# An output projection turned around: weights stationary, 512 tokens moving, split weights re-read from DRAM

## The chip, the cores and the metric

One Trainium2 chip, one core. The metric is device time in microseconds of one execution of the whole kernel. A run's time lies a little above the span that the profile shows (from the first to the last instruction).

## The reference

One decoder layer over 2048 tokens of width 1024, all in float32:

```
h   = rms_norm(x, g_mix)
mix = rwkv7_time_mix(h @ rw_in ...)          # 768 columns, a delta-rule scan over the tokens
mem = memory_cross_attention(q_mem, kv)      # 256 columns, 4 heads into 256 memory tokens
x   = x + concat(mix, mem) @ w_out           # the output projection: (2048 x 1024) @ (1024 x 1024)
u   = rms_norm(x, g_ffn) @ w_ff1
x   = x + square(relu(u)) @ w_ff2            # 1024 -> 4096 -> 1024
```

The change touches the line with `w_out` alone.

## The kernel before

A float32 product is made of three TensorE products. `split` (L89 to L96) writes an operand as a high part (ScalarE rounds it to fp32r, L92) and a low part (VectorE subtracts, L93); high by high, high by low and low by high are then summed in PSUM.

The tokens are in four groups of 512. The kernel has three stretches in time.

- `project` (L634) makes the input projection of a group: 22 blocks of 128 columns, each with 24 matmuls of 512 moving tokens (L102, PSUM tile `pz`), the weights being the stationary operand. Group 0 splits the weights and keeps both parts in DRAM (`w_d`); the later groups load the parts with four DMAs of 256 KB per block (L655). Six blocks of a group are turned back to token rows by four TensorE transposes (L688) and a copy (L690).
- The delta-rule scan works through 16 pairs of chunks of 64 tokens (`prepare`, `scan`, `post`); the result of a pair goes to the DRAM tile `mix_d` (L566). Beside it, as filler, run the projections of later groups, the cross-attention (`mem_attention`, result in `mem_d`), and the output projection `output` (L808). `dense` (L111) gives the filler's steps priorities that lie a few pairs behind the scan. From the priorities a planner writes the order of every engine before the kernel runs.
- The MLP (`prologue`, `layer1`, `layer2`) is dense TensorE work from about 1520 us to the end. The first `prologue` norms the rows of groups 0 and 1 and splits them into tiles that take the memory that the earlier stretches give back.

`output(g, parts)` loads the group's `mix_d` and `mem_d` rows (tile `mt`, L817 to L820) and splits them into `xh` and `xl` (one pair of tiles for each half of the 1024 inputs). For each quarter of 256 output columns, `weights256` (L612) loads four tiles of `w_out` (L617) and splits them into eight tiles `wo`. Then `rows_mm` (L624) makes, for each part of 256 tokens, 48 matmuls in which 128 tokens are the stationary operand and 256 weight columns move (L629, PSUM tile `pout`). The result has token rows already: VectorE adds `x` (L834) and one DMA stores it to `x2_d` (L835). Groups 0, 1 and 2 are done in one call with both parts; group 3 in two calls of one part each, behind pairs 13 and 15 of the scan. So each of the five calls loads and splits all of `w_out`: 16 DMAs of 256 KB and 32 splits.

Nearly all DMAs are issued from SyncE (SP), in one order; an issue that waits holds up those behind it. The pool of weight tiles has eight buffers (`WBUF`, 2 KB in each partition, so 256 KB a tile) and the pool of small tiles seven (`SLB`). The PSUM pool `psx` has three buffers.

Of the kernel before, what the change touches and what calls it, by code (L numbers as in the profile page):

```python
# [9 lines left out]
F32 = mybir.dt.float32  # L10
# [3 lines left out]
ALU = mybir.AluOpType  # L14
# [5 lines left out]
P = 128  # L20
T = 2048
D = 1024
KB = D // P
NG = 4
G = T // NG
# [10 lines left out]
WQ = 4  # L36
# [15 lines left out]
SPAN = list(zip(CUTS, CUTS[1:]))  # L52
# [8 lines left out]
def hybrid_layer(  # L61
# [6 lines left out]
    nc = tc.nc  # L68
    x = x[0]
# [3 lines left out]
    dram = ctx.enter_context(tc.tile_pool(name="dram", bufs=1, space=DRAM))  # L73
    cst = ctx.enter_context(tc.tile_pool(name="cst", bufs=1))

    ident = cst.tile([P, P], F32, name="ident")
# [12 lines left out]
    def split(src, hi, lo, gain=None):  # L89

        if gain is None:
            nc.scalar.copy(hi, src)  # L92
            nc.vector.tensor_tensor(lo, src, hi.bitcast(F32), op=ALU.subtract)  # L93
        else:
            nc.scalar.activation(hi, src, AF.Copy, scale=gain)
            nc.vector.scalar_tensor_tensor(lo, src, gain, hi.bitcast(F32), ALU.mult, ALU.subtract)  # L96

    def mm3_steps(ps, wh, wl, xh, xl, nk):

        for k in range(nk):  # L100
            for i, (a, b) in enumerate(((wh, xh), (wh, xl), (wl, xh))):
                nc.tensor.matmul(ps, a(k), b(k), start=(k == 0 and i == 0), stop=(k == nk - 1 and i == 2))  # L102
            yield
# [7 lines left out]
    def dense(first, last, *steps):  # L111

        kept = tc.cur_priority
        pos = lambda q: rank["base"] + (q + LAG) * PAIR_RANKS
        n = sum(c for _, c in steps)
        i = 0
        for s, c in steps:
            for j in range(c + 1):
                tc.cur_priority = int(pos(first) + (pos(last) - pos(first)) * min(1.0, (i + j) / n))
                if next(s, rank) is rank:  # L120
                    break
            else:
                raise AssertionError("more steps than told")
            i += c
        tc.cur_priority = kept

    def mixed(a, b, na, nb):

        b, due = iter(b), 0
        for s in a:  # L130
            yield s
            due += nb
            if due >= na:
                due -= na
                next(b, None)
        yield from b
# [8 lines left out]
    x2_d = [dram.tile([G, D], F32, name=f"x2_d{g}") for g in range(NG)]  # L145
# [27 lines left out]
    psx = xstk.enter_context(tc.tile_pool(name="psx", bufs=3, space=PSUM))  # L173
# [299 lines left out]
    def scan(d, S):  # L473
        states = []
        for c in range(2):
            e = d["ch"][c]
            AR, PT, WV, Z, BKT = (e[n] for n in ("AR", "PT", "WV", "Z", "BKT"))
            states.append(S)
            for q in range(2):
                nc.scalar.copy(bycol(WV[:C])[:, q], S[q * HD : (q + 1) * HD])  # L480
            rhs = pr.tile([P, NB, HD], F32, tag="rhs", name="rhs")
            pc = psc.tile([P, NB, HD], F32, tag="c", name="prhs")
            for h in range(NH):
                rs = slice((h % 2) * C, (h % 2) * C + C)
                nc.tensor.matmul(pc[rs, h // 2, :], PT[:, head(h), :C], WV[:, h * HD : (h + 1) * HD],  # L485
                                 start=True, stop=True)
            nc.scalar.copy(rhs, pc)
            pc = psc.tile([P, NB, HD], F32, tag="c", name="pw")
            for b in range(NB):
                for q in range(2):  # L490
                    nc.tensor.matmul(pc[q * C : (q + 1) * C, b, :], Z[:, b, q * C : (q + 1) * C], rhs[:, b, :],
                                     start=True, stop=True)
            for q in range(2):
                nc.scalar.copy(bycol(WV[:C])[:, q], pc[q * C : (q + 1) * C])
            pS = psc.tile([P, NB, HD], F32, tag="c", name="pS")
            for h in range(NH):
                rs = slice((h % 2) * HD, (h % 2) * HD + HD)
                nc.tensor.matmul(pS[rs, h // 2, :], BKT[:, h * HD : (h + 1) * HD],
                                 WV[:, h * HD : (h + 1) * HD], start=True, stop=True)
            Sn = st.tile([P, NB, HD], F32, tag="S", name="S")  # L500
            nc.vector.tensor_tensor(Sn, S, pS, op=ALU.add)
            nc.vector.tensor_tensor(Sn, Sn, bc(e["ec"]), op=ALU.mult)
            S = Sn
        return S, states
# [74 lines left out]
    last = [xp.tile([P, 20], F32, name=f"last{i}") for i in range(2)]  # L579

    w_d = [dram.tile([P, WQ, 2, KB // WQ, P], F32, name=f"w_d{b}") for b in range(NPB)]

    def small(shape, name, dt=F32):
        return ep.tile(shape, dt, tag="sl", name=name, bufs=SLB)

    def weights():

        n = KB // WQ
        w = [wp.tile([P, 2, n, P], F32R, tag="w", name="w") for _ in range(WQ)]
        return w, lambda k: w[k // n][:, 0, k % n, :], lambda k: w[k // n][:, 1, k % n, :]  # L590

    def operands(name):

        return [xp.tile([P, 4, G], F32R, tag=name, name=name, bufs=2) for _ in range(2)]
# [17 lines left out]
    def weights256(src, gain=None):  # L612

        w = []
        for k2 in range(KB // 2):
            ws = small([P, 2, 256], "ws")
            nc.sync.dma_start(ws, src[2 * k2 * P : (2 * k2 + 2) * P, :].rearrange("(k p) n -> p k n", p=P))  # L617
            for k in range(2):
                w.append(wp.tile([P, 2, 256], F32R, tag="w", name="wo"))
                kk = 2 * k2 + k  # L620
                split(ws[:, k], w[-1][:, 0], w[-1][:, 1], None if gain is None else gain[:, kk : kk + 1])
        return w

    def rows_mm(po, th, tl, w):  # L624

        for k in range(KB):
            for t in range(2):
                for i, (a, b) in enumerate(((th, 0), (th, 1), (tl, 0))):
                    nc.tensor.matmul(po[:, t, :], a(k, t), w[k][:, b],  # L629
                                     start=(k == 0 and i == 0 and t == 0),  # L630
                                     stop=(k == KB - 1 and i == 2 and t == 1))
            yield
# [175 lines left out]
    def output(g, parts=(0, 1)):  # L808

        mh, ml = operands("xh"), operands("xl")  # L810
        for h4 in range(2):
            for tt in [2 * t2 + i for t2 in parts for i in range(2)]:
                tsl = slice(tt * P, (tt + 1) * P)
                tc.cur_priority -= UPM
                mt = small([P, 4, P], "mt")
                if h4 == 0:
                    nc.sync.dma_start(mt, mix_d[g][:, :4, tsl])  # L817
                else:
                    nc.sync.dma_start(mt[:, :2, :], mix_d[g][:, 4:, tsl])
                    nc.sync.dma_start(mt[:, 2:, :], mem_d[g][:, :, tsl])  # L820
                split(mt, mh[h4][:, :, tsl], ml[h4][:, :, tsl])
                tc.cur_priority += UPM
        for qq in range(4):
            csl = slice(qq * 256, (qq + 1) * 256)
            w = weights256(w_out[0][:, csl])
            for t2 in parts:
                r0 = t2 * 256
                xr = small([P, 2, 256], "xr")
                nc.sync.dma_start(
                    xr, x[g * G + r0 : g * G + r0 + 256, csl].rearrange("(t p) c -> p t c", p=P))  # L830
                po = psx.tile([P, 2, 256], F32, tag="x", name="pout")
                yield from rows_mm(po, lambda k, t: mh[k // 4][:, k % 4, r0 + t * P : r0 + (t + 1) * P],
                                   lambda k, t: ml[k // 4][:, k % 4, r0 + t * P : r0 + (t + 1) * P], w)
                nc.vector.tensor_tensor(xr, xr, po, op=ALU.add)  # L834
                nc.sync.dma_start(x2_d[g][r0 : r0 + 256, csl].rearrange("(t p) c -> p t c", p=P), xr)  # L835


    def memory(*groups):
# [12 lines left out]
    for p in range(NPAIR):  # L851
        d = nxt
        S, states = scan(d, S)
        if p + 1 < NPAIR:
            nxt = prepare(p + 1)
        post(p, d, states)
        if p == 3:
            dense(*SPAN[3], (mixed(output(0), memory(3), 64, 24), 88))
        elif p in (7, 11):
            dense(*SPAN[p // 4 + 3], (output(p // 4), 64))  # L860
        elif p in (13, 15):
            dense(*SPAN[p // 2], (output(3, (p // 2 % 2,)), 32))
    tc.cur_priority = rank["base"] + 20 * PAIR_RANKS
    astk.close()
    bstk.close()
# [275 lines left out]
```

## Time and profile before

| | |
|---|---|
| median of 3 runs | 2777.49 us (2774.64 to 2781.78) |
| profiled execution, its own time | 2781.47 us |
| its span | 2779.8 us, mean granted TensorE clock 0.956 |
| input projection, scan and filler | 0 to about 1480 us |
| output projection's matmuls | 1075.7 to 1479.9 us |
| first matmul of the MLP | about 1520 us |
| matmuls of `layer1` and `layer2` back to back | 216 to 223 in each 50 us |

A row of a group of instructions gives the line, the engine, the operation, the tiles as out<-in, the shape and the count; behind the bar the busy time in us and the mean duration of one in ns; behind the second bar the idle time of the engine just before them and what ended it. Durations of matmuls include the way through the array, so matmuls that follow each other overlap: what one costs in a stream is the distance between the starts. The clock is the share of 2.4 GHz that TensorE was granted: 1.00 is 2.4 GHz and 0.50 is 1.2 GHz.

### The profile page before, as it was taken

How to read it: one execution, taken by the hardware profiler on the slowest of the kernel's cores; microseconds unless marked ns; L12 is line 12 of the kernel's file. 1: busy time of each engine (PE TensorE's matmuls, PEld its weight loads, DVE VectorE, ACT ScalarE, POOL GpSimd, SP SyncE). 2: the span in 40 equal slices, each digit the busy share in tenths (PEclk: the TensorE clock that was granted, in tenths of full speed). 3: DMA queues.
4: the chain of work that ended last, by engine and by line, in shares of the span. 5: the costliest groups of instructions: out<-in, count | busy, mean ns of one | idle time of the engine just before them, and what ended most of it. 6: DMA issues, size and time to landing. Idle time of an engine off the chain costs nothing.

```text
span 2779.8 us, 49460 instructions
## 1 busy us (share of the span) xinstructions
PE 2620.1 (94%) x17620; PEld 2131.9 (77%) x17620; DVE 1807.5 (65%) x4500; ACT 1410.8 (51%) x3053; POOL 413.1 (15%) x236
## 2 busy tenths in 40 slices
PE   6989999999899998997996999999999999999999
PEld 4777777777677777777885888878888888888887
DVE  4556657676866666778568777765875666655564
ACT  5564456465645547363446444444744444544443
POOL 2002133425304241333111000000100000000000
PEclk9999999999989988798997999999999999999999
DMA  8987564665454544335574576786775444456675
GB/s 251 286 263 215 166 176 135 168 174 165 135 152 138 144 126 120 100 86 164 160 241 133 201 260 244 275 306 191 246 258 170 145 144 155 150 192 208 211 252 167
DMA packets 468444, 519.35 MB, mean 187 GB/s; under 512 B 117538, under 2 KB 291682, under 8 KB 468196
## 3 DMA queue, kind: packets, MB, share of 16 engines
q1 hardware_dynamic: 468196, 516.18, 60.0%
q8 instruction: 139, 2.28, 0.3%
q14 instruction: 109, 0.89, 0.1%
HBM read 361.86 MB, written 154.14 MB: 186 GB/s over the span
## 4 chain that ended last, share of the span: by engine, by line
PE 74%; DMA 10%; DVE 9%; ACT 2%; issue 2%; SPq 2%; POOL 1%; DVEq 0%; ACTq 0%; POOLq 0%
PE pu L964 23%; PE py L1073 22%; PE pz L102 12%; PE pout L629 5%; PE pp L390 2%; DVE zt L431 1%; DVE Zw L435 1%; DMA zdr<-Zw 1%; PE prhs L485 1%; DMA qt<-q_d 1%; DMA KT<-rk_d 1%; DMA Z<-zdr 1%; DMA xt<-in_x_dram 1%; DMA ws<-in_rw_in_dram 1%; PE py L522 1%
## 5 line engine op out<-in xcount | busy, mean ns | idle before, releaser
L102 PE MATMUL pz<-xh,w 128*128 128x512 f32 x1408 | 484.9, 413 | 4.5 <-DVE last L681 2.7
L1073 PE MATMUL py<-wpl,hhh 128*128 128x512 f32 x896 | 349.3, 390 | 0.0
L1073 PE MATMUL py<-wph,hhl 128*128 128x512 f32 x896 | 348.3, 389 | 0.0
L1073 PE MATMUL py<-wph,hhh 128*128 128x512 f32 x896 | 344.0, 391 | 0.0
L102 PEld LDWEIGHTS pz<-xh,w 128*128 128x128 f32 x1408 | 268.9, 193 | 71.8 <-issue 6.6
L93 DVE TENSOR_TENSOR hhl<-hr,hhh 128x512 fp32r<-128x512 f32 x224 | 154.7, 691 | 225.6 <-ACT hhh L92 225.5
L92 ACT CAST hhh<-hr 128x512 fp32r<-128x512 f32 x224 | 139.1, 621 | 311.1 <-PE py L1073 295.5
L102 PE MATMUL pz<-xl,w 128*128 128x512 f32 x704 | 287.7, 409 | 0.4 <-DVE xl L93 0.4
L629 PE MATMUL pout<-wo,xh 128*128 128x256 f32 x1024 | 218.7, 307 | 18.9 <-DVE wo L93 9.6
L431 DVE TENSOR_TENSOR zt<-Ti,Zw 96x96 f32<-96x96 f32 (+20 forms) x736 | 171.2, 256 | 69.3 <-DMA Ti<-nd 49.7
L397 POOL TENSOR_TENSOR PT<-PT,msk 64x768 f32<-64x768 f32 x64 | 178.6, 2790 | 131.4 <-ACT PT L392 129.1
L629 PEld LDWEIGHTS pout<-wo,xh 128*128 128x128 f32 x1024 | 174.5, 205 | 28.9 <-DVE wo L93 12.3
L1073 PEld LDWEIGHTS py<-wph,hhl 128*128 128x128 f32 x896 | 168.4, 188 | 35.0
L1073 PEld LDWEIGHTS py<-wph,hhh 128*128 128x128 f32 x896 | 168.4, 188 | 34.8 <-DVE u L999 0.2
L1073 PEld LDWEIGHTS py<-wpl,hhh 128*128 128x128 f32 x896 | 168.4, 188 | 34.6
L435 DVE TENSOR_TENSOR Zw<-Zw,zt 96x96 f32<-96x96 f32 (+20 forms) x736 | 161.2, 242 | 6.7
L102 PEld LDWEIGHTS pz<-xl,w 128*128 128x128 f32 x704 | 135.8, 193 | 29.8 <-issue 1.9
L93 DVE TENSOR_TENSOR wpl<-wr,wph 128x512 fp32r<-128x512 f32 x224 | 153.3, 684 | 3.8 <-ACT wph L92 3.8
L629 PE MATMUL pout<-wo,xl 128*128 128x256 f32 x512 | 153.1, 299 | 0.0
L86 POOL TENSOR_TENSOR nr<-nm,nhalf 128x1 f32<-128x1 f32 x34 | 28.1, 827 | 789.2 <-DVE nm L84 736.3
L92 ACT CAST wph<-wr 128x512 fp32r<-128x512 f32 x224 | 138.2, 617 | 8.5 <-PE pu L964 7.5
L390 PE MATMUL pp<-AR,BK 64*128 64x128 f32 x768 | 94.5, 322 | 18.5 <-ACT PT L392 16.3
(293 smaller groups left out, 5640.5 us busy)
## 6 DMA issues: line engine op xcount, KB each, us to landing
w<-w_d SPq DMA_DIRECT2D x264, 256.0 KB, 4.0
hr<-hc_d SPq DMA_DIRECT2D x224, 256.0 KB, 2.8
ws<-in_w_ff_dram SPq DMA_DIRECT2D x32, 1024.0 KB, 5.7
hc_d<-hs SPq DMA_DIRECT2D x128, 256.0 KB, 2.2
wr<-t_d SPq DMA_DIRECT2D x128, 256.0 KB, 3.1
wr<-in_w_ff_dram SPq DMA_DIRECT2D x96, 256.0 KB, 3.0
w_d<-w SPq DMA_DIRECT2D x88, 256.0 KB, 4.2
ws<-in_w_out_dram SPq DMA_DIRECT2D x80, 256.0 KB, 4.3
```

The source lines that it names most:

```text
L86: nc.gpsimd.tensor_tensor(t1, t0, nhalf[: ssum.shape[0], :n], op=ALU.pow)
L92: nc.scalar.copy(hi, src)
L93: nc.vector.tensor_tensor(lo, src, hi.bitcast(F32), op=ALU.subtract)
L102: nc.tensor.matmul(ps, a(k), b(k), start=(k == 0 and i == 0), stop=(k == nk - 1 and i == 2))
L390: nc.tensor.matmul(pps[q][:, j, :], BK[c][rs, b, :], d["AR"][rs, b, :], start=True, stop=True)
L397: nc.gpsimd.tensor_tensor(PT[o : o + C, :, w:], PT[o : o + C, :, w:], K["msk"][o : o + C, w:].unsqueeze(1).to_broadcast([C, NH, 2 * C - w] ...
L431: nc.vector.tensor_tensor(zt[:, j0:j1, :nt], Ti[:, s, s + 1 :].unsqueeze(1).to_broadcast([96, j1 - j0, nt]), Zw[:, j0:j1, s : s + 1].to_br ...
L435: nc.vector.tensor_tensor(Zw[:, j0:j1, s + 1 :], Zw[:, j0:j1, s + 1 :], zt[:, j0:j1, :nt], op=ALU.add)
L485: nc.tensor.matmul(pc[rs, h // 2, :], PT[:, head(h), :C], WV[:, h * HD : (h + 1) * HD], start=True, stop=True)
L629: nc.tensor.matmul(po[:, t, :], a(k, t), w[k][:, b], start=(k == 0 and i == 0 and t == 0), stop=(k == KB - 1 and i == 2 and t == 1))
L964: nc.tensor.matmul(ps, a[u][:, k * P : (k + 1) * P], b[v][:, k, :], start=(first and k == 0 and i == 0), stop=(k == 3 and i == 2), skip_gr ...
L1073: nc.tensor.matmul(ps[bk], a[u][:, m * P : (m + 1) * P], b[v], start=(fresh and c == 0 and t == 0), stop=(c == NCH - 1 and t == 2), skip_g ...
```

## The change

`output` takes blocks of 128 output columns, as `project` does. The weights are the stationary operand and all tokens of the call move: 512 in groups 0 to 2, 256 in the two calls of group 3. The result has output columns in the partitions; ScalarE copies it to the tile `ot`, and TensorE transposes turn it back to token rows in the PSUM tile `pto`, four (or two) for each block, after the fourth step of the next block (`tail`). The add and the store work on 128 columns in place of 256. The call for group 0 splits `w_out` and stores both parts to a new DRAM tensor `wo_d`; the other four calls load the parts from there, four DMAs of 256 KB for each block. The last `dense` line is told 64 steps in place of 32.

```diff
+    wo_d = [dram.tile([P, WQ, 2, KB // WQ, P], F32, name=f"wo_d{b}") for b in range(KB)]
...
-        for qq in range(4):
-            csl = slice(qq * 256, (qq + 1) * 256)
-            w = weights256(w_out[0][:, csl])
-            for t2 in parts:
-                r0 = t2 * 256
-                xr = small([P, 2, 256], "xr")
-                nc.sync.dma_start(
-                    xr, x[g * G + r0 : g * G + r0 + 256, csl].rearrange("(t p) c -> p t c", p=P))
-                po = psx.tile([P, 2, 256], F32, tag="x", name="pout")
-                yield from rows_mm(po, lambda k, t: mh[k // 4][:, k % 4, r0 + t * P : r0 + (t + 1) * P],
-                                   lambda k, t: ml[k // 4][:, k % 4, r0 + t * P : r0 + (t + 1) * P], w)
-                nc.vector.tensor_tensor(xr, xr, po, op=ALU.add)
-                nc.sync.dma_start(x2_d[g][r0 : r0 + 256, csl].rearrange("(t p) c -> p t c", p=P), xr)
+        n, r0 = 256 * len(parts), 256 * parts[0]
+        tsl = slice(r0, r0 + n)
+        byrow = lambda a, b: a[:, b * P : (b + 1) * P].rearrange("(t p) c -> p t c", p=P)
+        tail = None
+        for b in range(KB):
+            w, wh, wl = weights()
+            if g == 0:
+                for i, t in enumerate(w):
+                    ws = small([P, KB // WQ, P], "ws")
+                    rows = slice(i * (KB // WQ) * P, (i + 1) * (KB // WQ) * P)
+                    nc.sync.dma_start(ws, w_out[0][rows, b * P : (b + 1) * P].rearrange("(k p) c -> p k c", p=P))
+                    split(ws, t[:, 0], t[:, 1])
+                    nc.sync.dma_start(wo_d[b][:, i], t.bitcast(F32))
+            else:
+                for i in range(WQ):
+                    nc.sync.dma_start(w[i].bitcast(F32), wo_d[b][:, i])
+            po = psx.tile([P, n], F32, tag="x", name="pout")
+            steps = mm3_steps(po, wh, wl, lambda k: mh[k // 4][:, k % 4, tsl], lambda k: ml[k // 4][:, k % 4, tsl], KB)
+            for k, _ in enumerate(steps):
+                if k == 4 and tail is not None:
+                    tail()
+                    tail = None
+                yield
+            ot = small([P, n], "ot")
+            nc.scalar.copy(ot, po)
+
+            def tail(b=b, ot=ot):
+
+                xr = small([P, n // P, P], "xr")
+                nc.sync.dma_start(xr, byrow(x[g * G + r0 : g * G + r0 + n], b))
+                pt = psx.tile([P, n // P, P], F32, tag="x", name="pto")
+                for t in range(n // P):
+                    nc.tensor.transpose(pt[:, t, :], ot[:, t * P : (t + 1) * P], ident)
+                nc.vector.tensor_tensor(xr, xr, pt, op=ALU.add)
+                nc.sync.dma_start(byrow(x2_d[g][r0 : r0 + n], b), xr)
+        tail()
...
-            dense(*SPAN[p // 2], (output(3, (p // 2 % 2,)), 32))
+            dense(*SPAN[p // 2], (output(3, (p // 2 % 2,)), 64))
```

## Rows read from the trace of the kernel before

**Rows 1.** The page: busy time by engine; the chain that ended last, by engine.

```profile
PE 2620.1 (94%) x17620; PEld 2131.9 (77%) x17620; DVE 1807.5 (65%) x4500; ACT 1410.8 (51%) x3053; POOL 413.1 (15%) x236
...
PE 74%; DMA 10%; DVE 9%; ACT 2%; issue 2%; SPq 2%; POOL 1%; DVEq 0%; ACTq 0%; POOLq 0%
```

**Rows 2.** Five stretches: busy us (count) of each engine, clock, DMA share, GB/s.

```profile
1050.00:1255.00 205.00, 185.40 (x1878) 156.19 (x1879) 144.45 (x459) 118.65 (x317) 61.34 (x29) 0.82 0.36 99
1255.00:1390.00 135.00, 117.98 (x1351) 108.32 (x1351) 93.86 (x276) 57.02 (x139) 39.06 (x17) 0.89 0.58 167
1390.00:1430.00 40.00, 37.04 (x306) 36.42 (x305) 24.61 (x48) 12.26 (x32) 9.76 (x6) 1.00 0.69 212
1430.00:1480.00 50.00, 46.33 (x372) 45.09 (x372) 29.49 (x73) 24.43 (x66) 0.00 (x0) 1.00 0.82 260
1480.00:1520.00 40.00, 14.93 (x68) 11.63 (x67) 37.23 (x60) 31.48 (x58) 6.48 (x7) 0.61 0.34 112
```

**Rows 3.** The same view, tile pout alone: PE, PEld, DVE.

```profile
1255.00:1390.00 135.00, 74.81 (x494) 67.75 (x495) 7.18 (x11) 0.89 0.58 167
1390.00:1430.00 40.00, 36.03 (x288) 34.68 (x287) 4.10 (x6) 1.00 0.69 212
1430.00:1480.00 50.00, 46.33 (x372) 45.09 (x372) 4.78 (x7) 1.00 0.82 260
```

**Rows 4.** Groups of instructions by line and shape, whole span.

```profile
L629 PE MATMUL pout<-wo,xh 128*128 128x256 f32 x1024 | 218.7, 307 | 18.9 <-DVE wo L93 9.6 <-ACT wo L92 8.6 <-ACT pe_m L781 0.3
...
L93 DVE TENSOR_TENSOR wo<-ws,wo 128x256 fp32r<-128x256 f32 x160 | 71.0, 477 | 28.6 <-ACT wo L92 27.8
...
L92 ACT CAST wo<-ws 128x256 fp32r<-128x256 f32 x160 | 59.2, 404 | 70.9 <-DMA ws<-in_w_out_dram 34.5 <-PE pout L629 27.7 <-DVE xr L834 6.6
...
L690 ACT COPY vt<-pv 128x512 f32<-128x512 f32 x24 | 14.0, 583 | 7.1 <-PE pv L688 6.7 <-DMA ws<-in_rw_in_dram 0.3
```

**Rows 5.** PE in order of time, 256 moving columns: start us, us, instructions.

```profile
1278.56 0.41 PE L629 MATMUL pout<-wo,xl 128*128 128x256 f32 x1
...
1279.20 0.41 PE L629 MATMUL pout<-wo,xl 128*128 128x256 f32 x1
...
1400.51 0.28 PE L629 MATMUL pout<-wo,xl 128*128 128x256 f32 x1
1400.63 0.40 PE L629 MATMUL pout<-wo,xh 128*128 128x256 f32 x2
1400.87 0.28 PE L629 MATMUL pout<-wo,xl 128*128 128x256 f32 x1
```

**Rows 6.** The same view, 512 moving columns in the input projection.

```profile
1035.94 0.39 PE L102 MATMUL pz<-xl,w 128*128 128x512 f32 x1
1036.17 0.62 PE L102 MATMUL pz<-xh,w 128*128 128x512 f32 x2
1036.63 0.40 PE L102 MATMUL pz<-xl,w 128*128 128x512 f32 x1
```

**Rows 7.** Line 688: duration min/median/max ns, first and last start us.

```profile
L688 PE MATMUL pv<-ident,sl x4: 272/272/273, 1007.6 to 1007.9; 128*128 128x128 f32 x4
```

**Rows 8.** Groups of line 629 at 1050:1255, at 1255:1390 and at 1390:1480, in turn.

```profile
L629 PE MATMUL pout<-wo,xh 128*128 128x256 f32 x256 | 65.8, 342 | 1.4 <-ACT wo L92 1.0 <-ACT pe_m L781 0.3
...
L629 PE MATMUL pout<-wo,xh 128*128 128x256 f32 x330 | 71.4, 309 | 10.9 <-DVE wo L93 7.4 <-ACT wo L92 3.4
...
L629 PE MATMUL pout<-wo,xh 128*128 128x256 f32 x440 | 81.9, 285 | 6.6 <-ACT wo L92 4.2 <-DVE wo L93 2.2
```

**Rows 9.** DMA at 1390:1480 in 40 slices; weight loads, us to landing, whole span.

```profile
GB/s 171 186 224 20 0 233 50 298 151 256 201 258 190 205 373 317 347 374 375 306 293 276 280 278 335 280 250 237 197 274 263 335 291 247 288 218 284 263 38 95
...
w<-w_d SPq DMA_DIRECT2D x264, 256.0 KB, 4.0
```

**Rows 10.** SP: line 655's issues (ns min/median/max); waits at 1050:1560; two issues.

```profile
L655 SPq DMA_DIRECT2D w<-w_d x264: 314/338/2384, 186.6 to 1031.8; - x132
...
SPq L835 <- DVE Zw L435: 49.8, 5, 12.6
...
1420.19 1.80 SPq L566 DMA_DIRECT2D mix_d<-mixT  x1
...
1446.07 1.09 SPq L817 DMA_DIRECT2D mt<-mix_d  x2
```

## The prediction

> **What bounds the kernel now.** First the page: TensorE is busy for 94% of the span and holds 74% of the chain that ended last [rows 1]. A share over the whole span hides stages, so next come the stretches in which the output projection runs [rows 2]. The reader is to see four things there. From 1050 to 1390 us, beside the scan, PE is idle for 19.6 + 17.0 = 36.6 us and runs at a mean clock of 0.82 and 0.89, so part of the time at 1.2 GHz. From 1390 to 1480 the scan's recurrence is over and PE does almost nothing but this projection: 288 + 372 = 660 of its matmuls in 90 us, busy 36.0 and 46.3 us [rows 3]. In the last 50 of these the DMA engines are at a share of 0.82 already, with 260 GB/s. And from 1480 to 1520 PE waits for a prologue that starts when the projection has ended and keeps VectorE busy for 37 of 40 us. So the end of the last call's matmuls is passed on one for one to the end of the kernel: the MLP behind it is not touched, nor is anything ahead of 1050. Pair 15's result is stored at 1420 and loaded at 1446 [rows 10]; the last call could begin earlier but is behind its predecessors, so the scan doesn't set the end, the queue of projection work does.
>
> **The change part by part.**
>
> *Matmuls.* Three matmuls with 256 moving columns start within 1400.51 to 1400.87, so 0.120 us each [rows 5]. Three with 512 columns start within 1035.94 to 1036.63, so 0.230 us [rows 6]. A call for groups 0 to 2 had 384 x 0.120 = 46.1 us and gets 192 x 0.230 = 44.2: 1.9 us less. The turned operands win next to nothing: two matmuls of 256 columns took 0.240 us, one of 512 takes 0.230. Added are 32 transposes a call; four of them start within 0.3 us [rows 7], so 0.1 us each, 3.2 us. Net +1.3 a call. For group 3 the matmuls stay 256 columns wide and as many (2 x 192); only 2 x 16 transposes come on top, +3.2. Group 0's 1.3 lie in a stretch with 19.6 us of idle PE; I charge groups 1 and 2: **+3** (bounds 0, if idle time of PE takes these too, and +8, if every call's are on the path; no gain, since 32 transposes outweigh what the wider form saves).
>
> *Splits.* 128 of 160 splits go: 128 x 0.477 = 61 us of VectorE and 128 x 0.404 = 52 us of ScalarE [rows 4]. ScalarE gets 24 copies of 512 columns at 0.583 [rows 4] and 16 of 256 columns, by the cast of that size 0.404: 20.5 us. Neither engine is the bound (VectorE 94 of 135 us, [rows 2]), so this counts only where PE waited for a split: 1.4 us in the first stretch, 10.9 in the second, 6.6 in the third [rows 8]. The first stays (group 0 still splits), the second goes, the third is inside the next term: **-11**. Bounds: -30, if VectorE's relief also removes the remaining idle and half of the low-clock loss of that stretch; 0, if loads, which land 4.0 us after their issue [rows 9], take the splits' place, or because a 512-wide matmul needs all four token tiles split before it can start, where the old form needed two.
>
> *Loads of group 3.* Each of its two calls loaded 4.19 MB of weights (16 x 256 KB) and will load 8.39 (32 x 256 KB), with the same 192 matmuls of 0.12 us to hide them: one block of 24 matmuls and two transposes takes 3.1 us, and brings 1.05 MB of weights and 0.26 MB of `x` and `x2_d`; that would need 420 GB/s. From 1430 to 1480 there were 260 GB/s at a share of 0.82, so 317 at a full share, and 13.0 MB [rows 2]. There will be 8.4 MB more, less 1.05, because the eight weight buffers that are filled ahead stand for 2.1 MB of loads where they stood for 1.05; so 20.4 MB are to be moved: 64 us at 317 GB/s, 54 at the best slice of 375 [rows 9], and 3 us for the last block's matmuls, copy, transposes and add. Against 50: +17 or +7. I take +13, a rate between, nearer to 317, because that is the mean of the very stretch. **+13** (bounds: +4, if PE stays the bound, 2 x 24.6 and 4.2 of the waits that are there now, [rows 8]; +18). Groups 1 and 2 load twice as much too, but a block of theirs lasts 24 x 0.23 + 0.4 = 5.9 us for 1.6 MB, 270 GB/s where nothing else runs on PE; that is covered. If the scan's DMAs fall on it, the cover is gone and the +18 holds.
>
> The Trainium skill, "DMA: Bandwidth & Descriptors", section "Specifications", gives about 358 GB/s as what one core gets from HBM. The slices at 373 to 375 lie above it, the mean of the stretch below. With 358 the term would be +10 in place of +13.
>
> *Group 0's stores and the queue.* Its call issues 32 loads, 32 stores, 8 loads of `x` and 8 stores, where it had 16 + 8 + 8: 48 more issues of 0.34 us [rows 10], 16 us of SP's time in about 180 us. Each new store waits for VectorE's low part, and behind it in SP's order wait the scan's loads and its `nd`, `zdr` and `Z` transfers, and so the next pair. Such a wait exists in the trace: line 835's store stood behind VectorE's `Zw` five times, 49.8 us in all [rows 10]. Below nothing is excluded, as nothing is taken away from the queue there. Bounds 0 and +20 (two such waits of 10 us on the scan's way); **+4**, nearer to nothing, because 19.6 us of PE's time in that stretch are idle already and most stores find their split long done.
>
> *Edits at nothing.* The copy to `ot` (0.58 us) is covered by the 12 matmuls of the next block ahead of the transposes (2.8 us, in group 3 1.4); without that cover PE would wait 0.6 us a block, 24 us in all. The add has the same elements. `pto` takes a third PSUM buffer of `psx`; with the attention of group 3 beside group 0 this can hold a `pout` back, and PE's next filler behind it; that is inside the +20. Steps told to `dense` only space the priorities.
>
> Sum: 3 - 11 + 13 + 4 = **+9 us**. The profiled execution took 2781.5 us, 4.0 above the median; so 2790.5 for its like, and a median of 2787.
>
> **The rivals.**
>
> *A, faster: the filler packs.* With the splits gone, VectorE and ScalarE are free for the pairs' own chains, and group 2's call moves forward into the idle 17 us and the low clock of 1255 to 1390. Its place is this stretch; it decides as soon as more than about 22 us come back there, or the loads of group 3 get 350 GB/s. For it: that stretch has the most waits for splits. Against it: those waits sum to 10.9 us only. It gives -26 + 4 + 7 = -15: 2762.
>
> *B, the transfers keep up.* Group 3's loads run at 350 to 375 GB/s, as in the best slices [rows 9], and start ahead: 3 - 11 + 7 + 1 = 0: 2777. Against it: such a rate held for five slices, 11 us, in a row.
>
> *C, SP's order.* Group 0's stores hold the scan, the full +20 in place of +4, the rest as forecast: +25: 2802. For it: the 49.8 us of [rows 10]; against it: the wait was for work that came late, not for the store.
>
> *D, the clock falls in group 3.* PE waits for each weight tile. Granted clock and idle go together here: at 1255 to 1390, idle for 17 us, the clock was 0.89; at 1480 to 1520, busy 15 of 40 us, 0.61 [rows 2]. At 1278.56 to 1279.20, after a stretch of such waits, three matmuls took 0.64 us, 0.213 each, 1.2 GHz [rows 5]. If half of group 3's 384 run so, that is 192 x 0.093 = 18 us more, partly under the loads: +9 + 18 = +27, so 2804. The Trainium skill names this as the bad loop, "TensorE: Matmul & The Clock Gate", section "Loop structure matters more than you think": a wait for a DMA between matmuls lets the clock drop. The trace agrees for long waits; none of its rows shows a wait of a few tenths of a microsecond between every six matmuls.
>
> **How the numbers follow.** Forecast 0.38 (own range +4 to +18), A 0.30, B 0.14, C 0.10, D 0.08. A measurement of this kernel tells 0.3%, 8.3 us, from no change. The forecast splits 0.25 slower and 0.13 within; A 0.27 faster and 0.03 within; B is within but for 0.01 faster; C and D are slower. So faster 0.28, same 0.29, slower 0.43. The range goes from 2758 (most of A, whose worst bound is -26) to 2808 (C and D): about 0.15 is left out.
>
> **What would show it.** Right: no wait of PE for `wo`; from the first to the last matmul of group 3's two calls some 62 us in place of 49, at 300 GB/s or more and PE busy for under 85%, its waits ended by loads from `wo_d`; 512-column matmuls 0.23 us apart. Wrong: group 3 at 0.12 us a matmul with its loads in time (B), the last call ended ahead of 1470 (A), a pair of the scan in 1075 to 1255 that takes 10 us longer behind an SP wait for a store (C), or a granted clock under 0.9 in group 3 (D). The whole prediction falls if the order before 1050 changes.

## The result and the profile after

The changed kernel took 2800.0 us (median of 4 runs, 2796.4 to 2806.1) beside 2776.8 for the kernel before: ratio 1.0083, 95% interval 1.0059 to 1.0107, 23 us slower. That lies in the predicted range (2758 to 2808), on the side called likeliest, but 13 us above the predicted 2787. The profiled execution took 2802.2 us with a span of 2800.5, 20.7 more than the span before.

The page again, answering [rows 1]: the engines' totals, and the shares of the chain that ended last.

```profile
PE 2624.1 (94%) x17172; PEld 2100.8 (75%) x17172; DVE 1759.8 (63%) x4380; ACT 1377.6 (49%) x2965; POOL 409.9 (15%) x236
...
PE 71%; DMA 11%; DVE 9%; ACT 3%; SPq 2%; issue 2%; POOL 1%; DVEq 0%; ACTq 0%; POOLq 0%
```

TensorE is busy for 4 us more in a span 21 us longer; VectorE and ScalarE lost 48 and 33 us of work, and PE's share of the chain fell. So what was added is mostly waiting. To see where, I cut both traces at the same events: the first matmul of group 0's call, the first of group 1's, the first of group 3's, and the end of the last `pout`. First the kernel before, then the one after (columns as in [rows 2]).

```profile
1075.70:1271.40 195.70, 177.19 (x1774) 149.78 (x1773) 140.75 (x474) 106.03 (x281) 67.66 (x30) 0.81 0.36 96
1271.40:1427.00 155.60, 143.46 (x1530) 134.50 (x1531) 101.89 (x273) 58.83 (x148) 41.62 (x22) 0.93 0.57 169
1427.00:1479.90 52.90, 47.87 (x385) 46.42 (x384) 31.38 (x76) 25.57 (x68) 0.00 (x0) 1.00 0.84 267
```

```profile
1074.20:1262.90 188.70, 165.07 (x1615) 128.49 (x1613) 141.96 (x467) 104.80 (x281) 64.05 (x30) 0.85 0.53 150
1262.90:1431.00 168.10, 151.28 (x1212) 119.33 (x1211) 74.43 (x214) 46.69 (x103) 43.60 (x22) 0.90 0.71 203
1431.00:1504.50 73.50, 57.93 (x414) 54.39 (x414) 10.60 (x21) 9.23 (x21) 0.00 (x0) 0.90 0.95 302
1505.00:1545.00 40.00, 16.66 (x68) 13.39 (x68) 36.74 (x60) 29.92 (x58) 6.24 (x7) 0.57 0.37 115
```

The reader is to see three things. Group 3's stretch (third line) grew from 52.9 to 73.5 us: PE's idle time there (its stretch less its busy time) went from 5.0 to 15.6 us, its clock from 1.00 to 0.90, and the DMA share to 0.95 at 302 GB/s. Groups 1 and 2 (second line) took 12.5 us more although the splits are gone, and group 0 (first line) 7.0 less. The prologue behind the projection (last line, answering the last of [rows 2]) is as it was. The whole difference of spans: -1.5 ahead of group 0, -7.0, +12.5, +20.6, +1.4 to the first MLP matmul, -5.3 in the MLP; together +20.7.

What PE waited for in group 3's stretch (engine, line, what it waited for; total us, times, longest):

```profile
PE pout L102 <- DMA mt<-mem_d: 7.1, 1, 7.1
PEld pout L102 <- DMA w<-wo_d: 6.7, 7, 3.4
PE pout L102 <- DMA w<-wo_d: 6.3, 8, 3.1
```

Each of these is a load. (A wait of 4.0 us for `xh`, the split of a row operand that had just landed, ends at 1430.96 with group 3's first matmul; it lies ahead of this stretch and counts to groups 1 and 2.) The 7.1 us are the start of the second call, whose operands `mt` were queued behind its predecessor's weight loads, as SP's order shows (start us, us, what was issued; SP issues a DMA only when its buffer is free):

```profile
1430.41 2.02 SPq L998 DMA_DIRECT2D ws<-in_w_ff_dram  x2
1433.15 5.10 SPq L839 DMA_DIRECT2D w<-wo_d  x6
...
1464.17 1.39 SPq L839 DMA_DIRECT2D w<-wo_d  x3
...
1466.95 1.08 SPq L818 DMA_DIRECT2D mt<-mix_d  x2
```

The first line is a collision that I had not in my sum: two loads of 1 MB for the MLP's first weights go out at 1430.4, as group 3's matmuls begin, just ahead of its weights. The kernel before issued the same two at 1419.1, 8 us ahead of its group 3. The chain of waits (start us, us, what held it) goes through these loads:

```profile
1433.15 9.29 DMA w<-wo_d
...
1455.42 5.67 DMA w<-wo_d
...
1464.17 4.45 DMA w<-wo_d
1468.64 4.62 DMA mt<-mem_d
1473.27 6.23 PE pout L102 x37
```

And PE in order of time, before and after such a wait:

```profile
1438.71 0.28 PE L102 MATMUL pout<-xl,w 128*128 128x256 f32 x1
1438.83 0.28 PE L102 MATMUL pout<-xh,w 128*128 128x256 f32 x1
...
1442.49 0.58 PE L102 MATMUL pout<-xh,w 128*128 128x256 f32 x1 [3.15 <-DMA w<-wo_d]
...
1443.51 0.41 PE L102 MATMUL pout<-xl,w 128*128 128x256 f32 x1
1443.72 0.41 PE L102 MATMUL pout<-xh,w 128*128 128x256 f32 x1
```

Before the wait the matmuls start 0.12 us apart (1438.71, 1438.83), after it 0.21 (1443.51, 1443.72): 1.2 GHz. By the granted clock and the distances of the starts, 10 to 11 us of matmuls in the stretch ran at that level, in three pieces, each behind one of the waits of 4.0, 3.15 and 7.1 us: 44 to 48 matmuls, which cost 4.1 to 4.5 us at 0.093 each (an estimate from the starts). Before, none did.

In the stretch of groups 1 and 2 the waits of PE: the two for the projection before, and the four longest after (`pe` is the scan's):

```profile
PE pout L629 <- DVE wo L93: 9.0, 6, 2.8
PE pout L629 <- ACT wo L92: 3.4, 1, 3.4
```

```profile
PE pout L102 <- ACT xh L92: 4.0, 1, 4.0
PE pout L102 <- DVE xr L857: 3.5, 1, 3.5
PE pe L466 <- ACT Z L467: 2.9, 1, 2.9
PE pout L102 <- DMA w<-wo_d: 2.2, 1, 2.2
```

The 12.4 us of split waits went as predicted (3.4 of them end with group 1's first matmul, just ahead of the stretch); 12.6 of others stand there now, 4.0 of them group 3's wait for its first rows. The operations' own prices came out as worked: three 512-wide matmuls start within 1397.92 to 1398.62, 0.23 us apart (as [rows 6]), and the transposes and copies have the durations of [rows 7] and [rows 4]:

```profile
1397.92 0.40 PE L102 MATMUL pout<-xl,w 128*128 128x512 f32 x1
1398.16 0.63 PE L102 MATMUL pout<-xh,w 128*128 128x512 f32 x2
1398.62 0.40 PE L102 MATMUL pout<-xl,w 128*128 128x512 f32 x1
```

```profile
L856 PE MATMUL pto<-ident,ot 128*128 128x128 f32 x128 | 22.0, 282 | 1.1 <-ACT ot L848 1.0 <-DVE xr L857 0.2
L848 ACT COPY ot<-pout 128x512 f32<-128x512 f32 x24 | 14.1, 587 | 45.9 <-PE pout L102 44.0 <-DMA x_d<-xr 1.9
```

### The profile page after: what moved, and what is told of

It reads as the page before. It is cut to its first block, busy times and chain, and to the rows that moved or that the text cites. A ratio compares the mean times of both kernels' runs of the same rounds, so it can differ in the third digit from the quotient of the medians.

```text
span 2800.5 us, 48524 instructions
## 1 busy us (share of the span) xinstructions
PE 2624.1 (94%) x17172; PEld 2100.8 (75%) x17172; DVE 1759.8 (63%) x4380; ACT 1377.6 (49%) x2965; POOL 409.9 (15%) x236
## 4 chain that ended last, share of the span: by engine, by line
PE 71%; DMA 11%; DVE 9%; ACT 3%; SPq 2%; issue 2%; POOL 1%; DVEq 0%; ACTq 0%; POOLq 0%
PE py L1097 22%; PE pu L988 19%; PE pz L102 12%; PE pout L102 4%; PE pp L390 2%; DVE zt L431 2%; DMA xr<-in_x_dram 1%; DVE Zw L435 1%; DMA ws<-in_w_ff_dram 1%; DMA w<-wo_d 1%; DMA ws<-in_rw_in_dram 1%; DMA zdr<-Zw 1%; PE prhs L485 1%; PE pw L491 1%; DMA xt<-in_x_dram 1%
## 5 line engine op out<-in xcount | busy, mean ns | idle before, releaser
L102 PEld LDWEIGHTS pz<-xh,w 128*128 128x128 f32 x1408 | 271.2, 194 | 73.5 <-issue 6.6
L102 PE MATMUL pout<-xh,w 128*128 128x512 f32 (+1 forms) x640 | 200.3, 388 | 26.5 <-DMA w<-wo_d 8.6
L397 POOL TENSOR_TENSOR PT<-PT,msk 64x768 f32<-64x768 f32 x64 | 176.5, 2758 | 128.7 <-ACT PT L392 126.4
L102 PEld LDWEIGHTS pout<-xh,w 128*128 128x128 f32 x640 | 122.9, 207 | 48.6 <-ACT xh L92 11.8
L102 PE MATMUL pout<-xl,w 128*128 128x512 f32 (+1 forms) x320 | 120.8, 378 | 0.0
L390 PE MATMUL pp<-AR,BK 64*128 64x128 f32 x768 | 90.6, 313 | 22.2 <-ACT PT L392 18.5
```

Of the source, the lines that this page charges most:

```text
L390: nc.tensor.matmul(pps[q][:, j, :], BK[c][rs, b, :], d["AR"][rs, b, :], start=True, stop=True)
L397: nc.gpsimd.tensor_tensor(PT[o : o + C, :, w:], PT[o : o + C, :, w:], K["msk"][o : o + C, w:].unsqueeze(1).to_broadcast([C, NH, 2 * C - w] ...
```

## The experiments

Each kernel is the changed one with one edit, and is compared with the kernel before on the same chip. The expectations name theories by letters; the chief ones are L (group 3's doubled loads are the loss) against F (the new form itself, with its transposes and late add, is the loss), and W (the wait for the row operands at a call's start). This table puts the outcomes side by side, in us of one profiled execution each; the stretches are cut as above, from the starts of the matmuls. Up to group 0's first matmul, with next to nothing edited ahead of it, these executions differ by up to 15.7 us (it comes between 1064.5 and 1080.2 us), so a few us in one row tell nothing by themselves.

| kernel | ratio to before | interval | groups 0-2 | group 3 |
|---|---|---|---|---|
| before | 1 | | 351.3 | 52.9 |
| after | 1.0083 | 1.0059-1.0107 | 356.8 | 73.5 |
| e1 old form in group 3 | 1.0012 | 0.9999-1.0025 | 353.0 | 59.4 |
| e2 half the bytes in group 3 | 1.0038 | 1.0022-1.0054 | 356.0 | 65.1 |
| e3 one call for group 3 | 1.0036 | 1.0022-1.0050 | 367.1 | 50.1 |
| e4 `x` early, all groups | 1.0110 | 1.0092-1.0128 | 370.2 | 71.1 |
| e5 shared row operands | 1.0064 | 1.0048-1.0079 | 356.1 | 76.0 |
| e6 split on chip in group 3 | 1.0187 | 1.0164-1.0210 | 353.6 | 105.3 |
| e7 e1 and `x` early | 1.0012 | 1.0000-1.0024 | 355.3 | 54.4 |
| e8 `x` early, not in group 0 | 1.0086 | 1.0068-1.0104 | 352.4 | 79.2 |
| e9 old form, stored in 1, 2 | 1.0023 | 1.0006-1.0039 | 354.4 | 60.6 |
| e11 old form, stored in 1-3 | 1.0048 | 1.0032-1.0064 | 353.3 | 67.6 |
| e12 e11, one call for group 3 | 1.0039 | 1.0025-1.0052 | 351.5 | 65.6 |
| e13 no transposes | 1.0066 | 1.0046-1.0087 | 352.5 | 77.7 |

**e1: group 3 in the old form.** Its weights are loaded as given and split on the chip, and `dense` is told 32 steps for it again; the rest is the changed kernel.

```diff
+        if g == 3:
+            for qq in range(4):
+                csl = slice(qq * 256, (qq + 1) * 256)
+                w = weights256(w_out[0][:, csl])
...
+            return
```

> Group 3's two calls keep the form of before (w_out loaded unsplit, split on the chip, 256 weight columns moving); groups 0 to 2 are as in the changed kernel. Theory L (the doubled weight bytes of group 3 fall into a stretch whose DMA engines are full): group 3's calls take 48 to 50 us again instead of 73, the last one ends near 1480, the time is that of before within 0.3% (2770 to 2785). Rival F (the new form itself, with its copy, transposes and late add, is slower in group 3): the same here, so this run doesn't tell L from F. Rival G (the loss is in groups 0 to 2): the time stays at 2795 or more.

2782.0 us against 2777.3. Of the 23 us, some 18 are gone, and the interval takes in no change at all. So most of the loss is in what was done to group 3. Its stretch:

```profile
1417.50:1476.90 59.40, 52.96 (x383) 51.01 (x384) 31.79 (x77) 25.90 (x67) 0.00 (x0) 0.90 0.85 264
```

PE is idle for 6.4 us in place of 15.6. The DMA rate, 264 GB/s, is that of before (267). This does not yet separate the bytes from the form.

**e2: half the bytes, new form.** Group 3 loads the high parts alone and uses them in place of the low parts too; as many loads, matmuls and transposes, half the weight bytes.

```diff
+                    if g == 3:
+                        nc.sync.dma_start(w[i][:, 0].bitcast(F32), wo_d[b][:, i, 0])
...
+                if g == 3:
+                    wl = wh
```

> As the changed kernel, but group 3 loads only the high parts of the split weights (128 KB a DMA in place of 256, as many DMAs) and uses them for the low parts too, so its low-part products are not those of the reference; count and size of the matmuls, copies, transposes and stores are the same. Theory L: the two calls take 50 to 56 us instead of 73, time 2778 to 2785. Rival F: they stay above 68 us, time 2795 or more. Rival Q (SP's issues are too many in too little time): no change either, since the issues are as many, 2795 or more.

2787.9 us against 2777.3, 1.0038: 12 of the 23 us come back by the bytes, with the form untouched.

```profile
1426.30:1491.40 65.10, 55.97 (x412) 53.88 (x413) 10.72 (x21) 9.30 (x21) 0.00 (x0) 0.90 0.78 230
```

The DMA share fell to 0.78 and PE's idle time to 9.1 us: 5.5 at the start of the second call, a wait for `mt`, and 3.3 in waits for `w`, which were 6.3. Another 3.9, for `xh`, end with the first call's first matmul. The clock stayed at 0.90. But the 65.1 us lie between what the two theories had (50 to 56, and above 68): the bytes are a part of the loss, and 0.0038 of the ratio is left with no more weight bytes than before.

**e3: one call for group 3**, after pair 15, so its weights are loaded once.

```diff
-        elif p in (13, 15):
-            dense(*SPAN[p // 2], (output(3, (p // 2 % 2,)), 64))
+        elif p == 15:
+            dense(*SPAN[7], (output(3), 64))
```

> Group 3 is projected in one call of 512 tokens behind pair 15, in the new form, so its weights are loaded once (8.4 MB less) and 512 columns hide each block's load. Theory L: the call takes 192 x 0.23 + 3.2 = 47 us of PE and some 7 us for its rows after pair 15's store at about 1430, so the last matmul is near 1484 and the time is 2778 to 2786. Rival F: the copies, transposes and adds are of the same elements, so the time stays above 2795. Rival W (the wait for pair 15 is what counts): nothing of group 3 runs before 1432, the time is 2800 or more.

```profile
1437.50:1487.60 50.10, 50.09 (x220) 40.40 (x220) 7.59 (x11) 6.58 (x11) 0.00 (x0) 0.95 0.70 210
```

With half the loads PE has no idle time left: 50.1 us. But the call can start only when pair 15 is done; PE waited 14.7 us in one piece for its `xh`, and most of that came back as the 10 us of the column "groups 0-2". 1.0036, and 2790.3 us, between what L (up to 2786) and F (above 2795) had.

**e4, e8 and e7: `x` ahead of the matmuls.** The load of `xr` moves from the tail to ahead of `pout`: in all groups (e4), in groups 1 to 3 (e8), in 1 and 2 with group 3 as in e1 (e7).

```diff
+            xr = small([P, n // P, P], "xr")
+            nc.sync.dma_start(xr, byrow(x[g * G + r0 : g * G + r0 + n], b))
             po = psx.tile([P, n], F32, tag="x", name="pout")
```

> As the changed kernel, but the load of the x rows is issued ahead of a block's matmuls, as before, not with its add. Theory L: nothing or up to 4 us less, 2796 to 2801, since the bytes are the same. Rival X (VectorE's add waits for the late x load, 24.5 us at 1390 to 1430 and 49.7 us behind it, and holds the PSUM tile and the scan's work behind it on VectorE): 10 us less or more, 2790 or under.

> The changed kernel with the x rows early in groups 1 to 3, late in group 0. Theory X: group 0's stretch is 188 to 190 us again, group 1's some 88 in place of 96; 2788 to 2793. Rival N: no change, 2797 to 2803. If group 0's stretch stays above 205 us, the small buffers are not the reason for its growth.

> Group 3 in the old form, groups 0 to 2 in the new one, and for groups 1 and 2 the x rows are loaded ahead of the block's matmuls. In the run with x early everywhere, group 0's stretch grew by 23 us and group 1's shrank by 8. Theory X (the late x load makes VectorE, and with it the scan, wait in groups 1 and 2; in group 0 it is the seven small buffers that are short): group 1 and 2 take 8 to 10 us less than in the run with the old form for group 3 alone, 2771 to 2776, under the kernel before. Rival N (the shrinking of group 1's stretch was only work that group 0's longer one had done already): 2780 to 2786.

e4 got slower: 1.0110. Its group 0 took 212.0 us in place of 188.7; e8, which leaves group 0 alone, took 189.7 there and is where the changed kernel is (1.0086). SP's longest waits for the store of `x2` (line 858) in group 0, first in the changed kernel, then in e4:

```profile
SPq L858 <- DVE zt L431: 19.1, 4, 10.5
...
SPq L858 <- DVE Zw L435: 5.4, 1, 5.4
```

```profile
SPq L858 <- DVE Zw L435: 20.8, 2, 13.7
SPq L836 <- DVE w L93: 13.8, 11, 3.3
...
SPq L858 <- DVE zt L431: 12.1, 1, 12.1
```

The store waits for an add that stands behind the scan's work (`zt`, `Zw`) on VectorE: 24.5 us in five waits, 32.9 in three in e4; and the stores of the split weights (line 836) wait for their splits 13.8 us, where the changed kernel has 6.3. What SP is to issue for the scan stands behind both. That fits the 23 us without proving it; why the early `xr` brings it on (a small buffer that is held longer is the guess) was not tried by itself. In groups 1 and 2 the move made no difference to the sum: e7 is e1. So the late `x`, the largest of VectorE's waits in that stretch of the changed kernel (36.0 us), costs nothing there that these runs show.

**e5: group 3's second call keeps the first one's operand buffers**, so that its rows can't be late behind buffers of their own.

```diff
+        if g == 3 and kept3:
+            mh, ml = kept3
```

> As the changed kernel, but the two calls of group 3 use one set of operand tiles (each fills its own half), so that the second call's rows can be loaded and split while the first one's matmuls run. Theory L: the DMA engines stay the bound of the two calls; the wait of 7 us for rows between the calls goes, 3 to 6 us less, 2794 to 2797. Rival W (the waits at the calls' starts are the loss, not the bytes): 10 us less or more, 2790 or under.

1.0064, within the interval of the changed kernel, and group 3 took 76.0 us. The wait at the second call's start did not go: it is one for `xh` now, 7.6 us where it was 7.1 for `mt` (the other 3.8 of the first line end with the first call's first matmul). The waits for `w` stayed:

```profile
PE pout L102 <- ACT xh L92: 11.4, 2, 7.6
...
PE pout L102 <- DMA w<-wo_d: 7.0, 6, 3.0
```

SP loads the second call's rows at 1466.15, where the changed kernel does at 1466.95: buffers of their own were not what held them, and they still stand behind the first call's weights in SP's order. So this run missed its aim, and theory W, that the waits at the starts are the loss, is not decided by it.

**e6: split on the chip in group 3, new form.** Half the bytes, the late add kept.

```diff
-            if g == 0:
+            if g in (0, 3):
...
+                    if g == 0:
+                        nc.sync.dma_start(wo_d[b][:, i], t.bitcast(F32))
```

> As the changed kernel, but group 3's two calls load w_out unsplit (128 KB a DMA, rows of 512 bytes) and split it on ScalarE and VectorE, as group 0 does, without the stores. Bytes as in the kernel before, form as in the changed one. Theory L: near the run with half the bytes, 2783 to 2792. Rival F (the new form costs): 2795 or more.

A plain miss: fewer bytes, and 1.0187, the slowest of all.

```profile
1426.80:1532.10 105.30, 68.48 (x413) 64.29 (x414) 35.14 (x85) 32.65 (x82) 0.00 (x0) 0.82 0.53 149
```

DMA is half idle (0.53) and so is nearly every engine. PE's and SP's longest waits:

```profile
PE pout L102 <- ACT w L92: 37.0, 17, 5.6
```

```profile
SPq L859 <- DVE xr L858: 42.0, 13, 6.1
```

SP holds the store of block b (line 859) until its add is done, and that add comes after the first two matmuls of block b + 1. The raw weights of block b + 2 stand behind that store. With a load, a split and then a matmul to follow, the ring closes. One turn of it: first matmul of a block at 1445.78, behind a wait for its split; transposes of the block before at 1446.13, their add at 1447.17, its store at 1447.61, four loads from 1448.08, and the next block's first matmul at 1451.03, again behind a wait for its split. In all 42.0 us of SP's time in 13 waits. The stored weights of the changed kernel need no split and no small buffer; that this is what spares them the ring was not tried. So the form is not free; by this trace its price here hangs on SP's order, but no run moved the store to show it.

**e9, e11, e12: the old form with stored weights.** No turned operands, no transposes, no late add. Group 0 stores its split tiles; groups 1 and 2 (e9, shown), or 1 to 3 (e11, with `if g > 0`), load them; e12 is e11 with one call for group 3.

```diff
+            if g in (1, 2):
+                w = [wp.tile([P, 2, 256], F32R, tag="w", name="wo") for _ in range(KB)]
+                for k in range(KB):
+                    nc.sync.dma_start(w[k].bitcast(F32), wo_d[qq][:, k])
```

> The kernel before with one half of the change alone: group 0 also stores its split weights, groups 1 and 2 load them instead of splitting again; tokens stay the stationary operand, 256 weight columns move, no copy, no transpose, x loaded ahead; group 3 splits on the chip as before. Theory K (what ate the gain of the dropped splits in groups 1 and 2 is the turned form: 3.3 us of transposes a call and the adds and copies on the way to the scan): groups 1 and 2 take 145 to 150 us together, where before took 156 and the changed kernel 168; time 2767 to 2774. Rival M (the split waits give way to waits for the loads whatever the form): 155 us or more, time 2775 to 2785.

> The same, with group 3's two calls loading the split weights too. Theory L (bytes are the bound of group 3's calls): they take 64 to 72 us in place of 53, with 256 weight columns moving and no transposes, DMA share over 0.9; 10 to 18 us above the run in which group 3 splits. Rival F (the turned form was the loss in group 3): 50 to 56 us.

> The same, with group 3 in one call of both parts behind pair 15, so that its split weights are loaded once: as many bytes as the kernel before loads for group 3, and no splits. Theory L: 48 to 52 us for group 3's matmuls, DMA no bound; they start 5 to 10 us later than before, as they wait for pair 15, and the time is 2768 to 2778. Theory that the start's wait counts for more: 2780 or more.

e9 and e11 differ in group 3's loads alone (bytes doubled, splits gone). First groups 1 and 2, then group 3 of e9, and PE's two longest waits of groups 1 and 2; then group 3 of e11 and its wait.

```profile
1270.70:1434.60 163.90, 145.26 (x1533) 135.82 (x1534) 75.31 (x218) 39.96 (x93) 44.80 (x23) 0.92 0.68 204
1434.60:1495.20 60.60, 51.52 (x394) 50.33 (x393) 32.54 (x78) 27.00 (x71) 0.00 (x0) 0.92 0.84 261
```

```profile
PE pout L630 <- DVE xr L843: 7.8, 1, 7.8
...
PE pout L630 <- DMA wo<-wo_d: 6.2, 4, 2.4
```

```profile
1428.10:1495.70 67.60, 52.64 (x395) 49.97 (x393) 9.76 (x15) 4.31 (x9) 0.00 (x0) 0.95 1.01 347
```

```profile
PE pout L630 <- DMA wo<-wo_d: 15.0, 13, 6.4
```

In the old form the doubled loads cost 7.0 us (67.6 against 60.6): the DMA engines are full (share 1.01), and 15.0 us of waits for stored weights stand where e9 had none in this stretch. This is L without F, but 7.0 us are less than the 10 to 18 that were expected, about a third of the 20.6, and the intervals of the two ratios overlap. And groups 1 and 2 of e9 took 163.9 us, 8.3 more than before, with 45 us less of VectorE's and ScalarE's work in the stretch (75.3 + 40.0 for 101.9 + 58.8) and no transposes to pay for: there is no gain in the dropped splits in the old form either. Waits of another kind stand in their place: 7.8 us for an add that itself waited 8.5 us for its load of `x`, and 6.2 for the stored weights. e12's one call took 65.6 us, hardly less than e11's two, though it loads half as much: 14.1 us of it are one wait of PE for pair 15's `xh`, in its middle. L's 48 to 52 us, and 2768 to 2778 for the whole, failed.

**e13: no transposes.** The add takes `ot` as it lies; what is added to `x` is not turned back.

```diff
-                for t in range(n // P):
-                    nc.tensor.transpose(pt[:, t, :], ot[:, t * P : (t + 1) * P], ident)
-                nc.vector.tensor_tensor(xr, xr, pt, op=ALU.add)
+                nc.vector.tensor_tensor(xr, xr, ot.rearrange("p (t c) -> p t c", c=P), op=ALU.add)
```

> The changed kernel without the 128 transposes back: the add takes the copy ot as it lies, so the rows of x2 are not those of the reference; loads, stores, matmuls, copies and adds are as many. Theory L (group 3 is bound by its loads, groups 0 to 2 by PE's work with waits in it): the 10.4 us that the transposes of groups 0 to 2 take on PE go in part, 4 to 8 us less, and group 3 keeps 68 to 74 us; time 2791 to 2797. Rival F (the transposes and what hangs on them are the loss in group 3): group 3 takes 60 us or less, time 2785 or under.

```profile
1429.00:1506.70 77.70, 56.60 (x384) 52.77 (x384) 10.82 (x22) 9.30 (x21) 0.00 (x0) 0.87 0.90 287
```

1.0066, so the transposes are worth 0.0017 of the ratio, some 5 us, and the intervals overlap. In the profiled execution groups 0 to 2 are 4.3 us shorter and group 3 is not (77.7): there PE waits for loads and rows in the time that the transposes had. So in group 3 F falls as far as it is the transposes; the copy and the late add are still in this kernel.

## Why the prediction came out as it did

*Group 3's loads, +13: right in mechanism, mis-sized; +20.6.* The signs came as written: 302 GB/s, waits ended by `wo_d`, PE 79% busy (57.93 of 73.5). And the stretch follows the bytes (e2 against the changed kernel, e11 against e9). But it took 73.5 us and not 62 to 63, and the 50 us that I set against these were a window's; the calls before took 52.9. Of the 20.6, 10.5 are idle time of PE and 10.1 more busy time: 3.1 of transposes (worked out as 3.2 for the two calls, and charged to no term) and 7.0 of matmuls, some 4 of these by the low clock. What the term had not:

- Bytes. I counted 20.4 MB; 302 GB/s for 73.5 us are 22.2. The two loads for the MLP, 2.1 MB, moved into the stretch: 7 us at that rate, an estimate. The nearest pair of runs has the same code for group 3: e8, with the two loads at its start, moved 22.9 MB in 79.2 us; e4, where they went out 15 us ahead, 20.2 MB in 71.1. But e4's first call also waited 11.8 us for its rows ahead of the stretch, so no run shows the price by itself.
- Rate. I chose one above the 317 of a full share; the stretch had 302 at a share of 0.95, which is 318 at a full one. The +17 worked out from 317 was nearer than the +13 that I took. The Trainium skill gives about 358 GB/s as the limit of one core from HBM ("DMA: Bandwidth & Descriptors", section "Specifications"). No stretch here averaged that much: e11 came nearest with 347, and the changed kernel's had 302.
- The order of the loads. A call's row operands stand behind its predecessor's weights: 7.1 us of wait at the second start, and 4.0 at the first, just ahead of the stretch. e5 shows that buffers are not what holds them; an order of SP with the rows ahead was not tried.
- Rival D, set up as an alternative, came beside the forecast in part: 44 to 48 matmuls at 1.2 GHz where it had 192. The Trainium skill's bad loop has a long DMA wait ahead of matmuls that then run cold ("TensorE: Matmul & The Clock Gate", section "Loop structure matters more than you think"); the trace agrees at the wait of 3.15 us shown above, behind which the matmuls are 0.21 us apart.

*Split waits, -11: the step that failed.* The waits went, the time did not: groups 1 and 2 took 168.1 us, where the sum had 155.6 - 11 + 3 = 147.6. I had taken waits in front of an engine that works through a queue of filler as time that comes back when they go. But other waits took their place, and PE's idle time in the stretch rose from 12.1 to 16.8 us. That is 4.7 of the 12.5; the rest is busy time. Worked out from the starts, the 64 transposes took 6.6 us, the projection's matmuls 3.1 less, and the scan's, 762 in both kernels, 4.0 more, at a mean clock of 0.90 in place of 0.93. With the 3.5 of transposes and matmuls taken off, some 9 us were lost where 11 were to be won. The 2.2 us for `w` are of the kind that the term's bound of 0 had named, loads in place of splits. Apart from e3 and e4, with a cause of their own, all kernels need 351 to 357 us for groups 0 to 2, and in the old form without splits (e9) it is the same. Rival A, in which the filler packs, fell with it. Pair 15's result was stored at 1420.19 [rows 10], 344.5 us after group 0's first matmul, and goes out at 1429.74 in the changed kernel, 355.5 us after it:

```profile
1429.74 0.58 SPq L566 DMA_DIRECT2D mix_d<-mixT  x1
```

So over groups 0 to 2 the scan came 11.0 us later. That by itself did not set the end: the result is loaded at 1466.95, 37 us after its store. What it held up is not shown.

*Matmuls and transposes, +3: right.* In group 1 the matmuls took 1.6 us less and the transposes 3.3 more (worked out from starts), +1.7 a call where the sum had +1.3; e13's one execution has 4 us less for groups 0 to 2. The copy to `ot` came at nothing too: the transposes waited 1.0 us for it in the whole kernel (line 856 above).

*Group 0's stores, +4: wrong in sign.* SP did wait for the new stores, 24.4 us in all at line 836, 6.3 of them for splits. But its waits at the store to `x2_d`, from which the term took nothing away, fell from 59.9 us (line 835 before) to 26.3 (line 858). The stretch got 7.0 us shorter and its clock rose from 0.81 to 0.85; e9 and e11, in the old form with stores, have 190.5 us there too, so it does not take the turned form. Which of these makes it shorter was not tried. Rival C fell; that SP's order can do what it feared is shown by e6, and perhaps by e4, with another store.

*Rival B, the transfers keep up,* fell: e11 held 347 GB/s for 67.6 us, and PE waited all the same.

So +13 became +20.6, the +3 and -11 of groups 1 and 2 became +12.5, and +4 became -7.0: 26.1, less the 5.4 that the rest won, is the 20.7 of the spans. The forecast's own range (to +18) missed the 23; the full range holds it because C and D reached up there, and because the -7.0, which no term had, offset part of the two terms that came out too high. That part is luck.

Left open: why the scan ends later (11 us here) once groups 1 and 2 have no splits, whether by the order of the filler, by the time at the low clock or by a wait that I did not find; how the part of group 3's loss that is not bytes divides among the form, SP's order and the MLP's loads; and the 5 us between e1 and the kernel before, which the interval does not tell from nothing.

## What to carry to other kernels

A split that is done once and stored costs twice the bytes each time it is read again; check that price in the stretch with the least matmul time to each loaded byte (here the half calls of group 3), not over the whole kernel. Waits on an engine that always has filler ready are not a sum that can be cashed: find what else would end late, and compare both traces between the same events before believing it. With one in-order issue queue, ask for each store how late its data comes, and what loads stand behind it.

## What the runs showed of the hardware

Rates: group 3's stretch moved 302 GB/s at a share of 0.95 in the changed kernel, with `x` and `x2_d` in 128 KB transfers, and 347 at 1.01 in e11, with 256 KB ones and the same 256 KB loads of weights. That the smaller pieces make the difference was not measured by itself. Clock: in the changed kernel the matmuls started 0.21 us apart after a wait of 3.15 us and 0.12 us apart ahead of it. And 48 + 33 us less of VectorE's and ScalarE's work, on engines at 65% and 51% [rows 1], came with no gain in time.
